# Second merge of an attention layer: kept branch weights, gates on GpSimd's queue, norm rows split between ScalarE and GpSimd

## The chip, the cores and the metric

The kernel runs on one core of one Trainium2 chip. The metric is the device time of one execution in microseconds (us). Three runs of the kernel before gave 1576.5, 1585.75 and 1576.89, median 1576.89. The profile is of one further execution of 1572.65 us.

## The reference

One layer over a sequence of 1024 rows with 1024 columns. It norms x, projects it, and runs two attentions of 8 heads each (a causal one with forget gates and one over chunks), whose outputs o_a and o_c have 512 columns each. What matters here is the part after that:

```python
merged = (jax.nn.sigmoid(gate_a) * (o_a @ w_br_fox[l])
          + jax.nn.sigmoid(gate_c) * (o_c @ w_br_chunk[l]))
mix = merged @ w_out[l]
x = _layer_norm(alpha * x + (1.0 + g1) * mix, ln1_g[l], ln1_b[l])
h = _layer_norm(x) * (1.0 + sc2) + sh2
...
```

Behind it follow an up-projection, a causal convolution of width 3, a gated product, a down-projection and a last norm. All is float32.

## The kernel before, in words

A float32 operand is held as a high and a low part, and a product is three matmuls: high by high, high by low, low by high (`mm3`, lines 192 to 194: L192, L193, L194). The tile framework's scheduler sets the order of each engine's instructions from the program, and adds the waits. A tile of a pool with `bufs=n` waits until the tile n allocations earlier under the same tag was read for the last time.

The sequence goes in two halves of 512 rows. Each half has a **merge** and a **mix**.

`merge(half)` makes the merged columns, transposed, in eight blocks c of 128 columns. A block has two branches (b=1, then b=0), each 12 matmuls into one PSUM bank `psb`: 24 per block, 192 per merge. Its weights are `brd[c]`, 1 MB in DRAM, loaded by `parted_w` (L904) as two transfers of 512 KB, the high parts into `wh` and the low parts into `wl`, every third time both into `ws`. Its gates are a tile of 512 KB, `sgl`, from `gd` (L914, two buffers). VectorE (DVE in the profile) multiplies each branch by its gate and so frees the bank (L921), adds the two (L927); ScalarE (ACT) rounds the sum to the high part `mh` (L930) and VectorE takes the low part `ml` (L931).

`mix(half)` multiplies the eight blocks, as k = 0 to 7, by the output weights `wod[k]` (again 512 KB twice): for four row tiles t of 128 rows two banks `psm` each, three matmuls per k and bank (L947 to L949), 192 in all. Banks for t = 0 to 2 come from the six that the merge uses in turn; those for t=3 are two others. The second mix does k=0 for all four t first, and then for each t the list k = 1, 2, 4, 5, 6, 7, 3. Behind each t, VectorE multiplies by g1 and adds alpha times the row tile of x, `xr` (L974, L975; `xr` is loaded at L965, four buffers).

`norms(half)` is the layer norm of the four row tiles: statistics (L119, L121), a small chain for the factor r (L123 to L132), then two VectorE operations over 128x1024: (x − mean) × l1g (L984) and × r + l1b (L985). GpSimd's queue (POOL) stores the row (`xd`, L987). Then the rows are normed once more for the FFN: statistics, and a scaling by ScalarE into `x2` (L139, L140). The norms of half 0 run beside merge 1, one step per block; those of half 1 behind mix 1. Behind mix 1 PE also turns the normed rows of half 0 (L997, `turned_0`) and starts the up-projection.

In merge 1 all loads are issued by SyncE's queue (SP): branch weights, gates, ln rows, and output weights for mix 1. GpSimd has only the `xd` stores and two loads of up-projection weights (L871) there. The pool `hap` holds `h_11` and `h_21`, sixteen tiles of 256 KB, which `turned_0` fills after merge 1; the space is unused until then.

Of the kernel before, what the change touches and what calls it, by code (L numbers as in the profile page):

```python
# [12 lines left out]
F32 = mybir.dt.float32  # L13
F32R = mybir.dt.float32r
AF = mybir.ActivationFunctionType
ALU = mybir.AluOpType
# [3 lines left out]
P = 128  # L20
# [3 lines left out]
KD = D // P  # L24
H = 512
# [19 lines left out]
def body(ctx, tc, a, out):  # L45
    nc = tc.nc
    ve, se, pe, po, sy = nc.vector, nc.scalar, nc.tensor, nc.gpsimd, nc.sync
    uid = [0]

    def nm(s):  # L50
        uid[0] += 1
        return f"{s}_{uid[0]}"

    def opened(**kw):
        cm = tc.tile_pool(reuse_waits="tile", **kw)
        return cm, cm.__enter__()
# [28 lines left out]
    gd = dram.tile([2, 16, P, H], F32, name="gd", tag="gd")  # L85
# [11 lines left out]
    brd = dram.tile([KD, 4, P, H], F32, name="brd", tag="brd")  # L97
# [17 lines left out]
    def norm_scale(src, n=2, st=None):  # L115
        if st is None:
            st = small.tile([P, n, 6], F32, name=nm("st"), tag=f"st{n}", bufs=4 if n == 2 else 1)
            for i in range(n):
                ve.bn_stats(out=st[:, i, :], in_=src[:, i * D // n : (i + 1) * D // n])  # L119
# [12 lines left out]
        ve.tensor_tensor(out=r, in0=y, in1=t, op=ALU.mult)  # L132
        return mv, r

    def normalise(dst, src, on_act=False, st=None):
        mv, r = norm_scale(src, 2, st)
        if on_act:
            b = small.tile([P, 1], F32, name=nm("nb"), tag="nb")
            ve.scalar_tensor_tensor(out=b, in0=mv[:, 0:1], scalar=-1.0, in1=r, op0=ALU.mult, op1=ALU.mult)  # L139
            se.activation(out=dst, in_=src, func=AF.Identity, scale=r, bias=b)  # L140
        else:
            ve.tensor_scalar(out=dst, in0=src, scalar1=mv[:, 0:1], scalar2=r, op0=ALU.subtract, op1=ALU.mult)
# [48 lines left out]
    def mm3(ps, wh, wl, xh, xl, start, stop):  # L191
        pe.matmul(ps, wh, xh, start=start, stop=False)  # L192
        pe.matmul(ps, wh, xl, start=False, stop=False)  # L193
        pe.matmul(ps, wl, xh, start=False, stop=stop)  # L194
# [530 lines left out]
    for u, (ip, _) in enumerate(plan):  # L725
# [5 lines left out]
        for n in range(8 * u, 8 * u + 8):  # L731
            ip, i, g = steps[n]
# [73 lines left out]
    def operands(pool, name):  # L806
        return [[pool.tile([P, H], F32R, name=f"{name}{c}{k}", tag=f"{name}{c}{k}") for c in range(2)] for k in range(4)]

    ha_cm, hap = opened(name="ha", bufs=1)
    h_11, h_21 = operands(hap, "ha"), operands(hap, "hb")  # L810
    mxp = ctx.enter_context(tc.tile_pool(name="mxp", bufs=6, space=PSUM, reuse_waits="tile"))
    mxt_cm, mxt = opened(name="mxt", bufs=2, space=PSUM)
    mxb_cm, mxb = opened(name="mxb", bufs=2)
# [81 lines left out]
    if True:  # L895
# [3 lines left out]
        def parted_w(src, pool=None):  # L899

            tags = ("wh", "wl") if pool or next(sets) % 3 < 2 else ("ws", "ws")
            parts = [(pool or wp).tile([P, 2, H], F32R, name=nm(g), tag=g) for g in tags]
            for x, j in zip(parts, (2, 0)):
                sy.dma_start(out=x.bitcast(F32), in_=src[j : j + 2].rearrange("j p n -> p j n"))  # L904
            return parts

        def merge(half, os_, beside, ahead=iter(())):
            ms = []
            held = {}

            def branch(c, b):
                if c not in held:
                    sg = mx.tile([P, 2, H], F32, name=nm("sgl"), tag="sgl", bufs=2)
                    sy.dma_start(out=sg, in_=gd[half, 2 * c : 2 * c + 2].rearrange("b p s -> p b s"))  # L914
                    held[c] = [x.rearrange("p j (k n) -> p (j k) n", k=4) for x in parted_w(brd[c])], sg
                (bh, bl), sg = held[c]
                ps = mxp.tile([P, H], F32, name=nm("psb"), tag="mm")
                for k in range(4):
                    kk = 4 * b + k
                    mm3(ps, bh[:, kk, :], bl[:, kk, :], os_[kk][0], os_[kk][1], k == 0, k == 3)  # L920
                ve.scalar_tensor_tensor(out=sg[:, b, :], in0=sg[:, b, :], scalar=1.0, in1=ps, op0=ALU.add, op1=ALU.mult)  # L921

            for c in range(KD):
                branch(c, 1)
                branch(c, 0)
                sg = held.pop(c)[1]
                ve.tensor_tensor(out=sg[:, 0, :], in0=sg[:, 0, :], in1=sg[:, 1, :], op=ALU.add)  # L927
# [3 lines left out]
                ve.tensor_sub(out=ml, in0=sg[:, 0, :], in1=mh)  # L931
                ms.append((mh, ml))
                next(ahead, None)
                next(beside, None)
            return ms
# [44 lines left out]

        def norms(half, xs, xn):
            for t, xx in enumerate(xs):
                mv, r = norm_scale(xx)
                ve.scalar_tensor_tensor(out=xx, in0=xx, scalar=mv[:, 0:1], in1=l1g, op0=ALU.subtract, op1=ALU.mult)  # L984
                ve.scalar_tensor_tensor(out=xx, in0=xx, scalar=r, in1=l1b, op0=ALU.mult, op1=ALU.add)  # L985
                yield
                po.dma_start(out=xd[4 * half + t], in_=xx)  # L987
            for xx in xs:
                x2 = mxb.tile([P, D], F32, name=nm("x2"), tag="x2", bufs=4)
                normalise(x2, xx, True)  # L990
                xn.append(x2)
                yield

        def turned(tiles, j, psp=mxt, tag="tt"):
            ps = psp.tile([P, H], F32, name=nm("pst"), tag=tag)
            for t in range(4):
                pe.transpose(ps[:, t * P : (t + 1) * P], tiles[t][:, j * P : (j + 1) * P], ident)  # L997
            h32 = mxb.tile([P, H], F32, name=nm("h32"), tag="h32", bufs=4)
            se.activation(out=h32, in_=ps, func=AF.Identity, scale=modc[:, 4 * KD + j : 4 * KD + j + 1],
                          bias=modc[:, 3 * KD + j : 3 * KD + j + 1])  # L1000
            return h32

        def put(dst, x, y=None, op=None, e=(ve, ve, po), pool=mxb, n=2):
            if y is not None:
                t = pool.tile([P, H], F32, name=nm("ht"), tag="ht", bufs=n)
                e[0].tensor_tensor(out=t, in0=x, in1=y, op=op)
                x = t
            (e[1].copy if e[1] is se else e[1].tensor_copy)(out=dst[0], in_=x)
            e[2].tensor_sub(out=dst[1], in0=x, in1=dst[0])
            return x  # L1010

        def turned_0(tiles):
# [22 lines left out]
        l1g = mx.tile([P, D], F32, name="l1g", tag="l1g", bufs=1)  # L1035
        l1b = mx.tile([P, D], F32, name="l1b", tag="l1b", bufs=1)
# [19 lines left out]
            pass  # L1056
        o_cm.__exit__(None, None, None)
        hd_cm, hdp = opened(name="hd", bufs=2, side="right")
        turning = turned_0(x0)
        xs1 = mix(1, m1, iter(()), wide, turning, hdp)  # L1060
        for _ in turning:
# [227 lines left out]
    with tc.tile_pool(name="dn", bufs=2, reuse_waits="tile") as dn:  # L1289
# [44 lines left out]
        for p in products:  # L1334
            ps = bank_b if p in ("P5", "P3", "P2") else bank_a
# [117 lines left out]
```

## Time and profile before

| | |
|---|---|
| median of three runs | 1576.89 us |
| profiled execution | 1572.65 us |
| its span, first to last instruction | 1570.9 us |
| TensorE busy, share of the span | 96% |
| VectorE, ScalarE, GpSimd | 69%, 45%, 41% |
| mean granted TensorE clock | 0.990 |
| merge 0 and mix 0 | 730 to 817 us |
| merge 1 | 817.1 to 870.2 us |
| mix 1 | 870.2 to 916.1 us |

A matmul row's duration is from its start to a modelled end, and matmuls overlap: the pace is read from the distance of the starts. Operations of VectorE overlap by some tens of nanoseconds too. A bracket behind a row is the idle time before it on its engine, and what ended that. For a DMA, the row on its queue is only the issue; the time from issue to landing stands apart. PE is TensorE's matmuls, PEld its weight loads.

### The profile page before, as it was taken

The numbers are of one execution on the slowest core, as the hardware profiler recorded it, in microseconds if no ns is written. First come the engines' busy times: TensorE is split into PE (matmuls) and PEld (weight loads), VectorE is DVE, ScalarE is ACT, GpSimd is POOL, SyncE is SP. The second block draws the span as 40 slices with busy tenths as digits, with TensorE's granted clock in tenths as the row PEclk, the third lists the DMA queues.
The fourth block names the chain that finished last, engine by engine and source line by source line (L and its number), as shares of the span: only waits on it lengthen the run. The fifth ranks groups of instructions, "written<-read, shape, count | busy, mean of one in ns | idle before, by whom it ended". The sixth has DMA issues, their size and how long they took to land.

```text
span 1570.9 us, 21838 instructions
## 1 busy us (share of the span) xinstructions
PE 1509.7 (96%) x7663; PEld 1268.5 (81%) x7663; DVE 1081.9 (69%) x2161; ACT 708.2 (45%) x1316; POOL 641.5 (41%) x579
## 2 busy tenths in 40 slices
PE   6999989999999999899998999999999999999996
PEld 3788788889888888788886887888888888788885
DVE  6747566567757676564449488677778876845798
ACT  3545444554445454342102256445454454555451
POOL 0038988888788876100000003545445453000000
PEclk9999999999999999999999999999999999999999
DMA  9156665756666788426999676344333332697552
GB/s 370 40 168 221 216 207 198 233 194 201 220 202 201 253 280 273 172 99 228 307 339 336 242 255 207 104 173 155 133 121 120 129 112 103 223 342 256 196 187 76
DMA packets 130399, 317.81 MB, mean 202 GB/s; under 512 B 12897, under 2 KB 21809, under 8 KB 130289
## 3 DMA queue, kind: packets, MB, share of 16 engines
q1 hardware_dynamic: 94192, 207.79, 39.5%
q0 software_dynamic: 24432, 88.88, 16.6%
q10 hardware_dynamic: 11664, 19.75, 3.4%
q8 instruction: 60, 0.98, 0.3%
q14 instruction: 51, 0.41, 0.1%
HBM read 223.73 MB, written 84.25 MB: 196 GB/s over the span
## 4 chain that ended last, share of the span: by engine, by line
PE 80%; DVE 9%; DMA 7%; issue 2%; ACT 1%; SPq 0%; DVEq 0%; ACTq 0%
PE psu L852 24%; PE pso L502 4%; PE psd L1270 4%; PE psd L1271 4%; PE psd L1269 4%; PE pst L488 3%; PE psg L192 3%; PE psg L193 3%; PE psg L194 3%; PE psq L193 3%; PE psq L194 3%; PE psq L192 3%; DMA cb<-in_rel_t 2%; PE pss L434 2%; PE pss L435 2%; PE psv L295 2%
## 5 line engine op out<-in xcount | busy, mean ns | idle before, releaser
L852 PE MATMUL psu<-hc,wx 128*128 128x512 f32 x792 | 185.7, 389 | 0.1
L852 PEld LDWEIGHTS psu<-hc,wx 128*128 128x128 f32 x792 | 148.6, 188 | 31.4 <-ACT u L1195 0.5
L1118 DVE SCALAR_TENSOR_TENSOR pcv<-u,convp,pcv 128x1024 f32<-128x1024 f32 x88 | 113.2, 1286 | 45.4 <-ACT pcv L1116 44.5
L454 ACT ACTIVATE s<-s,mx 128x640 f32<-128x640 f32 (+7 forms) x128 | 94.5, 738 | 78.6 <-DVE mx L448 77.0
L1259 DVE TENSOR_TENSOR op<-rw,op 128x512 fp32r<-128x512 f32 x146 | 93.3, 688 | 52.9 <-ACT op L1258 52.6
L1258 ACT CAST op<-rw 128x512 fp32r<-128x512 f32 x146 | 85.2, 623 | 84.3 <-PE psd L1271 40.8
L1270 PE MATMUL psd<-op,op 128*128 128x512 f32 x292 | 113.6, 389 | 1.0 <-DVE op L1259 1.0
L1271 PE MATMUL psd<-op,op 128*128 128x512 f32 x292 | 113.6, 389 | 0.0
L491 ACT CAST pt<-pst 128x512 fp32r<-128x512 f32 (+1 forms) x192 | 82.5, 450 | 68.8 <-PE pst L488 67.3
L1269 PE MATMUL psd<-op,op 128*128 128x512 f32 x292 | 113.1, 389 | 0.0
L987 POOL DMA_DIRECT2D xd<-xr x8 | 4.3, 542 | 263.1 <-DVE xr L985 263.1
L192 PE MATMUL psq<-h1h,wh 128*128 128x512 f32 x256 | 104.4, 409 | 1.7 <-DVE h1h L188 1.3
L492 DVE TENSOR_TENSOR pt<-pst,pt 128x512 fp32r<-128x512 f32 (+1 forms) x192 | 96.5, 519 | 13.2 <-ACT pt L491 11.3
L192 PE MATMUL psg<-h1h,wh 128*128 128x512 f32 x256 | 104.6, 409 | 0.0
L194 PE MATMUL psg<-h1h,wl 128*128 128x512 f32 x256 | 100.6, 393 | 1.5 <-DVE wl L112 1.5
L194 PE MATMUL psq<-h1h,wl 128*128 128x512 f32 x256 | 101.2, 395 | 0.9 <-DVE wl L112 0.9
L193 PE MATMUL psq<-h1l,wh 128*128 128x512 f32 x256 | 101.5, 396 | 0.0
L193 PE MATMUL psg<-h1l,wh 128*128 128x512 f32 x256 | 100.7, 393 | 0.0
L502 PE MATMUL pso<-pt,vs 128*128 128x256 f32 x608 | 93.2, 292 | 6.4 <-DVE pt L492 6.2
L550 POOL TENSOR_SCALAR dr<-dr,cond 128x512 f32<-128x512 f32 x56 | 95.7, 1711 | 5.1 <-DMA dr<-in_w_ada 4.1
L502 PEld LDWEIGHTS pso<-pt,vs 128*128 128x128 f32 x608 | 82.9, 194 | 15.2 <-DVE pt L492 8.5
L488 PE MATMUL pst<-ident,s 128*128 128x128 f32 x528 | 83.7, 275 | 8.9 <-DVE pt L492 8.7
(284 smaller groups left out, 4013.7 us busy)
## 6 DMA issues: line engine op xcount, KB each, us to landing
ws<-in_w_up SPq DMA_DIRECT2D x34, 512.0 KB, 3.8
dr<-in_w_ada POOLq DMA_DIRECT2D x32, 512.0 KB, 4.7
dr<-in_w_down POOLq DMA_DIRECT2D x22, 512.0 KB, 5.2
td<-dr POOLq DMA_DIRECT2D x22, 512.0 KB, 5.4
rw<-td SPq DMA_DIRECT2D x44, 256.0 KB, 4.6
yd<-y SPq DMA_DIRECT2D x20, 512.0 KB, 2.8
rw<-yd SPq DMA_DIRECT2D x40, 256.0 KB, 4.6
rw<-sd SPq DMA_DIRECT2D x33, 256.0 KB, 4.6
```

The costliest lines, as they stand in the source:

```text
L192: pe.matmul(ps, wh, xh, start=start, stop=False)
L193: pe.matmul(ps, wh, xl, start=False, stop=False)
L194: pe.matmul(ps, wl, xh, start=False, stop=stop)
L488: pe.transpose(ps[:, b * P : (b + 1) * P], st[:, c0 : c0 + P], ident)
L492: ve.tensor_sub(out=dl, in0=src, in1=dh)
L502: pe.matmul(ps[:, 0:256], vs[:, h % 2, j0 + j, :], pt[j // 4][:, c, j % 4, :], start=j == 0 and c == 0, stop=j == nj - 1 and c == 1)
L550: po.tensor_scalar_mul(x[:, k % 2, :] if k else acc, x[:, k % 2, :], cond[:, k : k + 1])
L852: pe.matmul(ps, w[:, a_, k, :], h[k][b_], start=first, stop=k == 3 and a_ == 1, skip_group_check=on)
L1118: ve.scalar_tensor_tensor(out=ps, in0=u[b][:, 2 - d : S + 2 - d], scalar=cp[:, 2 - d : 3 - d], in1=ps, op0=ALU.mult, op1=ALU.add)
L1269: pe.matmul(ps[t], g[:, 0, ts], d[:, 0], start=start, stop=False, skip_group_check=on)
L1270: pe.matmul(ps[t], g[:, 0, ts], d[:, 1], start=False, stop=False, skip_group_check=on)
L1271: pe.matmul(ps[t], g[:, 1, ts], d[:, 0], start=False, stop=stop, skip_group_check=on)
```

## The change

Three things are changed, all around merge 1.

1. **Branch weights of blocks 4 to 7 are kept.** In merge 0 they are loaded as sixteen tiles `kw` of 256 KB (new function `kept_w`, L915) into the space of `h_11` and `h_21`, whose allocation moves behind merge 1. Merge 1 uses them again, and takes the blocks in the order 4, 5, 6, 7, 0, 1, 2, 3. Only blocks 0 to 3 are loaded again there.
2. **Gates of merge 1** are issued by GpSimd's queue instead of SyncE's (L926).
3. **Norm rows:** for the four tiles of half 0 and the first two of half 1, ScalarE now applies mean and factor in one operation (`normalise` with `on_act`), and GpSimd multiplies by l1g and adds l1b, two operations of 128x1024 (L1001, L1002). The last two tiles of half 1 stay on VectorE as before (L1005, L1006).

```diff
-    h_11, h_21 = operands(hap, "ha"), operands(hap, "hb")
+    kept = {}
...
+        def kept_w(c):
+
+            if c not in kept:
+                kept[c] = []
+                for i, j in enumerate((2, 0)):
+                    kept[c].append([])
+                    for b in range(2):
+                        x = hap.tile([P, H], F32R, name=nm("kw"), tag=f"h{'ab'[c % 2]}{i}{2 * b + c // 2 % 2}")
+                        sy.dma_start(out=x.bitcast(F32), in_=brd[c, j + b])
+                        kept[c][i].append(x.rearrange("p (k n) -> p k n", k=4))
+            return kept[c]
+
...
-                    sy.dma_start(out=sg, in_=gd[half, 2 * c : 2 * c + 2].rearrange("b p s -> p b s"))
-                    held[c] = [x.rearrange("p j (k n) -> p (j k) n", k=4) for x in parted_w(brd[c])], sg
+                    (po if half else sy).dma_start(out=sg, in_=gd[half, 2 * c : 2 * c + 2].rearrange("b p s -> p b s"))
+                    if c >= 4:
+                        held[c] = kept_w(c), sg
+                    else:
+                        held[c] = [[x[:, j].rearrange("p (k n) -> p k n", k=4) for j in range(2)]
+                                   for x in parted_w(brd[c])], sg
...
-            for c in range(KD):
+            for c in (4, 5, 6, 7, 0, 1, 2, 3) if half else range(KD):
...
         def norms(half, xs, xn):
             for t, xx in enumerate(xs):
-                mv, r = norm_scale(xx)
-                ve.scalar_tensor_tensor(out=xx, in0=xx, scalar=mv[:, 0:1], in1=l1g, op0=ALU.subtract, op1=ALU.mult)
-                ve.scalar_tensor_tensor(out=xx, in0=xx, scalar=r, in1=l1b, op0=ALU.mult, op1=ALU.add)
+                if half == 0 or t < 2:
+                    normalise(xx, xx, True)
+                    po.tensor_tensor(out=xx, in0=xx, in1=l1g, op=ALU.mult)
+                    po.tensor_tensor(out=xx, in0=xx, in1=l1b, op=ALU.add)
+                else:
+                    mv, r = norm_scale(xx)
+                    ve.scalar_tensor_tensor(out=xx, in0=xx, scalar=mv[:, 0:1], in1=l1g, op0=ALU.subtract, op1=ALU.mult)
+                    ve.scalar_tensor_tensor(out=xx, in0=xx, scalar=r, in1=l1b, op0=ALU.mult, op1=ALU.add)
                 yield
                 po.dma_start(out=xd[4 * half + t], in_=xx)
...
+        h_11, h_21 = operands(hap, "ha"), operands(hap, "hb")
         turning = turned_0(x0)
```

How it moves instructions is seen at two places. First GpSimd's queue during merge 1. Row tiles t = 0 to 3 of half 0 are xr_8663, xr_8665, xr_8667, xr_8669; before, its part there is

```order
L987 DMA xd<-xr_8663 128x1024 [waits DVE_49]
L987 DMA xd<-xr_8665 128x1024 [waits DVE_49]
L987 DMA xd<-xr_8667 128x1024 [waits DVE_49]
L987 DMA xd<-xr_8669 128x1024 [waits DVE_49]
L871 DMA sgl_9505<-in_w_up 128x1024 [waits DMASW1_49,DMASW0_49,DVE_49]
```

and now, from the fifth gate on (sgl_8919, sgl_8979, sgl_9042 and sgl_9105 are the gates of blocks 0, 1, 2 and 3; the first four gates and all of tile 0 stand ahead):

```order
L1001 TENSOR_TENSOR xr_8665<-xr_8665,l1g 128x1024 [waits DMAHW2_49,Activation_49]
L926 DMA sgl_8919<-gd 128x2x512 [waits DMASW6_49,DMASW1_49,DVE_49]
L1002 TENSOR_TENSOR xr_8665<-xr_8665,l1b 128x1024 [waits Pool_49]
L1008 DMA xd<-xr_8665 128x1024 [waits DMASW2_49,Pool_49]
L1001 TENSOR_TENSOR xr_8667<-xr_8667,l1g 128x1024 [waits DMAHW2_49,DMAHW1_49,Activation_49]
L1002 TENSOR_TENSOR xr_8667<-xr_8667,l1b 128x1024 [waits Pool_49]
L1001 TENSOR_TENSOR xr_8669<-xr_8669,l1g 128x1024 [waits DMAHW6_49,Activation_49]
L1008 DMA xd<-xr_8667 128x1024 [waits DMASW3_49,Pool_49]
L1002 TENSOR_TENSOR xr_8669<-xr_8669,l1b 128x1024 [waits Pool_49]
L926 DMA sgl_8979<-gd 128x2x512 [waits DMASW7_49,DVE_49]
L926 DMA sgl_9042<-gd 128x2x512 [waits DMASW1_49,DVE_49]
L926 DMA sgl_9105<-gd 128x2x512 [waits DMASW4_49,DVE_49]
```

The gates of blocks 1, 2 and 3 now stand behind the work on all four rows. Second, VectorE at the end of merge 1: before, the row operations of the last tile stand between the evictions of a block (sgl_8923 is the gate tile of the fifth block),

```order
L921 SCALAR_TENSOR_TENSOR sgl_8923<-sgl_8923,psb_8929 128x512 [waits DMAHW5_49,PE_49]
L931 TENSOR_TENSOR ml_8901<-sgl_8865,mh_8900 128x512 [waits Activation_49]
L123 TENSOR_SCALAR v_8910<-mv_8908 128x1 [waits DVE_49]
L127 RECIPROCAL y_8914<-sd_8912 128x1 [waits Activation_49]
L984 SCALAR_TENSOR_TENSOR xr_8669<-xr_8669,mv_8908,l1g 128x1024
```

and now, behind the fifth block's low part (ml_8955), the second norm's statistics wait for GpSimd's last row, and the evictions of blocks 1, 2 and 3 follow in a row:

```order
L947 TENSOR_TENSOR ml_8955<-sgl_8919,mh_8954 128x512 [waits Activation_49]
L139 SCALAR_TENSOR_TENSOR nb_9039<-mv_9026,r_9037 128x1 [waits DVE_49]
L121 BN_AGGR mv_9089<-st_9086 128x2
L119 BN_STATS st_9145<-xr_8669 128x6 [waits Pool_49]
...
L937 SCALAR_TENSOR_TENSOR sgl_8979<-sgl_8979,psb_8985 128x512 [waits DMASW4_49,PE_49]
L937 SCALAR_TENSOR_TENSOR sgl_8979<-sgl_8979,psb_8999 128x512 [waits PE_49]
L943 TENSOR_TENSOR sgl_8979<-sgl_8979 128x512 [waits DVE_49]
L947 TENSOR_TENSOR ml_9015<-sgl_8979,mh_9014 128x512 [waits Activation_49]
L937 SCALAR_TENSOR_TENSOR sgl_9042<-sgl_9042,psb_9048 128x512 [waits DMASW6_49,PE_49]
```

VectorE no longer does the row operations, but it now waits for GpSimd in their place, and block 3's gate needs the buffer that ml_9015 frees.

More of the change, by code (lines that the diff above doesn't have):

```diff
@@ L905, in parted_w @@
             return parts
+        def kept_w(c):
[8 more added lines that the diff above has]
+            return kept[c]
         def merge(half, os_, beside, ahead=iter(())):
-            ms = []
+            ms = {}
             held = {}
@@ L918, in branch @@
                 for k in range(4):
-                    kk = 4 * b + k
-                    mm3(ps, bh[:, kk, :], bl[:, kk, :], os_[kk][0], os_[kk][1], k == 0, k == 3)
+                    oh, ol = os_[4 * b + k]
+                    mm3(ps, bh[b][:, k, :], bl[b][:, k, :], oh, ol, k == 0, k == 3)
                 ve.scalar_tensor_tensor(out=sg[:, b, :], in0=sg[:, b, :], scalar=1.0, in1=ps, op0=ALU.add, op1=ALU.mult)
-            for c in range(KD):
+            for c in (4, 5, 6, 7, 0, 1, 2, 3) if half else range(KD):
                 branch(c, 1)
@@ L931, in merge @@
                 ve.tensor_sub(out=ml, in0=sg[:, 0, :], in1=mh)
-                ms.append((mh, ml))
+                ms[c] = (mh, ml)
                 next(ahead, None)
```

## Prediction

> **What bounds the kernel now.** I read the windows first, cut at the first and last matmul of each stage around the change: merge 0 with mix 0, merge 1, mix 1. Columns: window, length, then busy time and count of each engine, granted clock, DMA share, GB/s.
>
> ```profile
> core 0: us, PE busy (x) PEld busy (x) DVE busy (x) ACT busy (x) POOL busy (x), PEclk, DMA share, GB/s
> 817.09:870.18 53.09, 47.64 (x194) 37.38 (x192) 46.84 (x114) 12.20 (x20) 2.72 (x5) 0.94 0.93 342
> 870.18:916.12 45.94, 45.65 (x210) 37.57 (x209) 26.84 (x53) 10.21 (x18) 1.61 (x3) 1.00 0.59 218
> 730.00:817.00 87.00, 87.00 (x385) 72.03 (x385) 35.85 (x48) 9.77 (x13) 0.00 (x0) 1.00 0.98 320
> ```
>
> Merge 0 and mix 0 keep PE busy without a break: 385 matmuls in 87.00 us, 0.226 us each. Merge 1 has 192 of the same matmuls, 43.5 us at that pace, and takes 53.09: **9.6 us are lost there**, the only stage of the three that loses much. Next the matmul rows of merge 1 around each gap (start, time, operation, in brackets the idle time and its releaser):
>
> ```profile
> 845.54 0.39 PE L193 MATMUL psb<-ol,wh 128*128 128x512 f32 x1
> 847.44 0.50 PE L194 MATMUL psb<-oh,wl 128*128 128x512 f32 x1 [1.51 <-DMA wl<-brd]
> ...
> 857.82 0.39 PE L194 MATMUL psb<-oh,wl 128*128 128x512 f32 x1
> 860.74 0.47 PE L192 MATMUL psb<-oh,ws 128*128 128x512 f32 x1 [2.52 <-DVE st L119]
> ...
> 861.83 0.63 PE L193 MATMUL psb<-ol,ws 128*128 128x512 f32 x1
> 863.43 0.80 PE L194 MATMUL psb<-oh,ws 128*128 128x512 f32 x1 [0.98 <-DMA ws<-brd]
> ...
> 865.73 0.63 PE L193 MATMUL psb<-ol,ws 128*128 128x512 f32 x1
> 866.16 0.63 PE L194 MATMUL psb<-oh,ws 128*128 128x512 f32 x1
> ...
> 868.14 0.39 PE L192 MATMUL psb<-oh,ws 128*128 128x512 f32 x1
> ...
> 870.18 0.39 PE L947 MATMUL psm<-wh,mh 128*128 128x512 f32 x1
> 872.90 0.39 PE L947 MATMUL psm<-wh,mh 128*128 128x512 f32 x1
> ```
>
> And SyncE's queue, which issues these weights (start, time in the queue):
>
> ```profile
> 852.96 0.43 SPq L904 DMA_DIRECT2D ws<-brd  x1
> 857.76 0.36 SPq L914 DMA_DIRECT2D sgl<-gd  x1
> 858.22 0.42 SPq L904 DMA_DIRECT2D ws<-brd  x1
> ```
>
> The three gaps, start to start less one matmul, are 1.67, 2.69 and 1.17 us, with some tenths at 823: about 6.3. All are branch weights that come late; the 2.52 is put down to DVE, but the first matmul of `ws` starts 7.8 us after that load's issue at 852.96, so it is the load again. The remaining 3 us are pace: after the gaps matmuls start 0.43 apart instead of 0.23, until 868.1. So the stage is bound by 8 MB of branch weights, 4 MB of gates and the loads beside them, at a DMA share of 0.93.
>
> **The change, part by part.**
>
> *Weights kept.* Blocks 4 to 7 need no load in merge 1: 4 of its 8 MB are gone, and the other four blocks, now last, are asked for early. All gaps above go, and the half pace behind them. Merge 1's matmuls would end at 817.09 + 43.5 = 860.6, **−9.6 us**, if nothing else held them. The same loads in merge 0 become 16 of 256 KB instead of 8 of 512 KB: the bytes are equal, eight more issues at about 0.4 us each stand in SyncE's queue, and PE is covered there by weights that arrive ahead. I take 0, and the uncovered price for the third rival.
>
> *Gates behind GpSimd's work.* In merge 1 a gate tile is now issued by GpSimd's queue, which also does the four rows' scaling and adding. In GpSimd's order the gate of block 1 stands behind all eight of these operations, and those of 2 and 3 behind it. An eviction of a block needs its gate, and mix 1 needs the banks: t=2's first matmul (872.90 above) waits until block 3's product is evicted. So the chain is: tile 0 scaled by ACT, eight GpSimd operations and four issues, block 1's gate, its evictions, block 3's gate into the same buffer, its eviction, t=2. Rows for its terms:
>
> ```profile
> 829.94 0.15 DVE L132 TENSOR_TENSOR r<-y,t 128x1 f32<-128x1 f32 x1
> ...
> L984 DVE SCALAR_TENSOR_TENSOR xr<-xr,mv,l1g 128x1024 f32<-128x1024 f32 x4 | 5.1, 1271 | 0.0
> L140 ACT ACTIVATE x<-xr,nb,r 128x1024 f32<-128x1024 f32 x4 | 5.0, 1242 | 4.4 <-DVE nb L139 4.4
> L927 DVE TENSOR_TENSOR sgl<-sgl 128x512 f32<-128x512 f32 x8 | 5.5, 682 | 0.0
> L921 DVE SCALAR_TENSOR_TENSOR sgl<-sgl,psb 128x512 f32<-128x512 f32 x16 | 10.7, 675 | 5.9 <-PE psb L194 3.1 <-DMA sgl<-gd 2.8
> L931 DVE TENSOR_TENSOR ml<-sgl,mh 128x512 fp32r<-128x512 f32 x7 | 4.8, 689 | 0.3
> L987 POOL DMA_DIRECT2D xd<-xr x4 | 2.2, 547 | 208.7 <-DVE xr L985 208.7
> ```
> ```profile
> L553 POOL TENSOR_TENSOR acc<-acc,dr 128x512 f32<-128x512 f32 x56 | 73.5, 1313 | 1.5
> ```
> ```profile
> sgl<-gd SPq DMA_DIRECT2D x16, 512.0 KB, 5.9
> dr<-in_w_ada POOLq DMA_DIRECT2D x32, 512.0 KB, 4.7
> ```
> ```profile
> DMA to landing us min/median/max: 3.6/5.9/10.5
> ```
>
> No 128x1024 operation of two tensors on GpSimd stands in this trace. The nearest row is the same operation over 512 columns, 1313 ns. Twice that is 2.63. From below: VectorE's step from 512 to 1024 columns is 675 to 1271 ns, a factor of 1.88, which gives 2.47. From above: such an operation of GpSimd takes 1.75 instead of 1.29 in the stretch where VectorE works on two SBUF operands at once,
>
> ```profile
> 978.86 1.75 POOL L841 TENSOR_TENSOR wl<-s,wl 128x512 fp32r<-128x512 f32 x1
> ...
> 983.51 1.29 POOL L841 TENSOR_TENSOR wx<-wt,wx 128x512 fp32r<-128x512 f32 x1
> ```
>
> so 3.5. I take **2.63**, since the 1313 is a mean over 56 in company of a working VectorE. The working: tile 0's factor is there at 830.1; ACT takes it after the cast in its way, about 832.0, and needs 1.24: 833.2. Eight operations are 21.0, four issues of 0.55 are 2.2: block 1's gate is issued at 856.4. The landing was 5.9 from SyncE's queue in a crowded stretch and 4.7 for the same size from GpSimd's: I take 5.3, 861.7. Two evictions, the sum, ACT's cast and the low part, with VectorE operations starting 0.60 apart, are 3.1: the buffer is free at 864.8. Issue 0.2, landing 5.3, eviction 0.7: **t=2 starts at 871.0, 1.9 us before its 872.90 of now**. The 9.6 us thus shrink to 1.9: what was bought in weights is spent waiting for gates.
>
> *Pace after the wait.* Between 860.6 and 871.0 PE has only the first two row tiles of mix 1, 12 matmuls, 2.7 us. That is an idle stretch longer than those of now, after which matmuls ran at half pace from 861.4 to 868.1, 13 or 14 of them at 0.2 us extra each: **+2.7 us** here, at the start of the rest of mix 1. The Trainium skill, "TensorE: Matmul & The Clock Gate", Part 1, says that the clock halves after an idle window of about 3.4 us and returns after 3.4 us of work; an estimate by it is 1.7 us lost, so the sum would be −0.7 instead; the trace already shows half pace after a gap of 2.5.
>
> *Mix 1's own wait* is a weight that is late in the queue behind the branch weights,
>
> ```profile
> 883.10 0.50 PE L948 MATMUL psm<-wl,mh 128*128 128x512 f32 x1 [0.29 <-DMA wl<-wod]
> ```
>
> start to start 0.7, less one matmul: **−0.5**.
>
> *VectorE* loses eight operations of 1.27 in half 0 (10.2 us) and gains four of 0.15, but its operations on two SBUF tensors may slow beside GpSimd:
>
> ```profile
> L838 DVE TENSOR_TENSOR wt<-ws,ws x14: 677/1651/1781, 979.4 to 1305.8; 128x512 f32<-128x512 f32 x14
> ```
>
> 677 ns at best, 1651 in the middle (minimum/median/maximum). Two of these per block (sum, low part) over five blocks are at most 10 × 1.0 us. The two nearly cancel, VectorE has 6 us of slack in the stage, and GpSimd is done before the links of the chain that run on VectorE: 0. The Trainium skill, "GPSIMD Engine Reference", sections 1 and 3.1, speaks against the move: GpSimd shares its SBUF interface with VectorE instructions of two SBUF inputs, and an addition of two tensors over 2048 columns took 4497 ns. An estimate from that for 1024 is 2.25 us alone; the sum would be −2.7. The rows here are slower for their size than that.
>
> *SyncE* loses eight gate issues from merge 1, but the row loads of half 1 now wait for ACT to have read a tile that GpSimd finished, and the weights of k=1 and k=2 of mix 1 are queued behind them. GpSimd ends its last tile at about 856, statistics and ACT take it to 860; before, these weights went out at
>
> ```profile
> 870.14 0.87 SPq L904 DMA_DIRECT2D ws<-wod  x2
> ```
>
> so they are earlier all the same: 0.
>
> *Half 1.* Four VectorE operations go (two row tiles),
>
> ```profile
> 901.11 1.26 DVE L984 SCALAR_TENSOR_TENSOR xr<-xr,mv,l1g 128x1024 f32<-128x1024 f32 x1
> ...
> 909.34 1.23 DVE L985 SCALAR_TENSOR_TENSOR xr<-xr,r,l1b 128x1024 f32<-128x1024 f32 x1
> ```
>
> all under mix 1's matmuls, which end at 916. What PE waits for later comes from the last row tile, still on VectorE. From 0 to 5 us could be in it if these tiles became late on GpSimd; it has 2.6 × 2 each and nothing else to do. I take 0.
>
> **Sum** against the profiled execution (1572.65): −1.9 + 2.7 − 0.5 = +0.3, so 1573.0. Its median of three runs, 1576.89, lies 4.2 above: **1577 us**, no change. About 1% (15.8 us) is what a measurement of this kernel can tell from none, and no case below reaches it on its middle value.
>
> **The rivals.**
>
> *The gates come in time.* GpSimd at 2.47 ends 1.3 us earlier, and with less traffic both gates could land in the 3.6 of the fastest: −3.4. Then t=2 starts at 866.3, 6.6 before now; with the 0.5 of mix 1 that is −7.1, or 1570; without any half pace. If ACT comes earlier by 1 to 2 us as well, −9, 1568. For it: the DMA share falls with 4 MB less. Against it: GpSimd's eight operations are a fixed row, and even block 1's gate cannot be issued before 855.
>
> *Slower: GpSimd and VectorE get in each other's way.* At 3.5 each, eight operations take 28.0, 7.0 more than forecast; every microsecond of them goes on to block 1's gate: t=2 at 878.0, sum +7.3, **1584**. With slow landings of about 7.5 twice, 4.4 more: 1588. It decides from where GpSimd's operation passes 2.63: the forecast stands at no change, so each 0.1 us above costs 0.8. For it: the 1.75 row and VectorE's 1651. Against it: VectorE reads PSUM in half its work here, and the 1313 is a mean taken in company.
>
> *The change doesn't do what it says*: the kept loads, twice as many issues, come too late in merge 0, whose DMA share is already 0.98. Eight further issues of 0.42 are 3.4 us in the queue, and with a half pace after the gap about +5: 1582 with the forecast's rest. Against it: PE never waits there now.
>
> **How the numbers follow.** Forecast 0.45 (its own range 1573 to 1581); gates in time 0.25; slower by contention 0.2; stalls in merge 0, 0.1. The range from 1567 to 1588 takes in their ends. Over 1% faster would be below 1561, more than all that merge 1 loses, 0.02; over 1% slower, above 1592.7, needs GpSimd operations of 4.6 us, 0.03; within, 0.95.
>
> **What would show it.** Right: merge 1 has no wait for brd; GpSimd's 128x1024 operations take 2.5 to 2.7; the first matmul of t=2 starts within 2 us of 871 after a wait for a VectorE eviction that itself waited for a gate; half-pace matmuls follow. Wrong: t=2 starts before 868 (gates free), after 874 (contention), or merge 0 shows waits for `kw`; or the stretch behind 916 moves by more than 2 us.

## The result and the profile after

The changed kernel takes 1587.66 us, the median of 20 runs (1575.97 to 1599.25), against 1576.76 for the kernel before, also of 20: ratio **1.0079, 95% interval 1.0054 to 1.0103**, slower by 8.5 to 16 us. The forecast was no change. Its profiled execution took 1579.61 us with a span of 1577.5, 6.6 more than the 1570.9 of before.

The windows of the change, cut as those of before (merge 1, the wait behind it, mix 1; the last number of a row is GB/s, the share ahead of it that of the DMA engines, then the granted clock):

```profile
core 0: us, PE busy (x) PEld busy (x) DVE busy (x) ACT busy (x) POOL busy (x), PEclk, DMA share, GB/s
816.16:864.06 47.90, 45.63 (x193) 36.83 (x191) 46.95 (x96) 13.67 (x20) 25.43 (x17) 0.96 0.57 198
864.06:870.32 6.26, 0.15 (x2) 0.03 (x1) 5.11 (x13) 3.13 (x4) 0.74 (x1) 0.73 1.02 400
870.32:923.35 53.03, 49.78 (x208) 38.91 (x209) 25.94 (x53) 12.55 (x20) 11.88 (x8) 0.93 0.57 211
```

From the first matmul of merge 1 to the end of mix 1 (called the **stage** from here on) it took 99.0 us before (817.09 to 916.12) and 107.2 now (816.16 to 923.35). Merge 1 is 5.2 shorter, 6.3 of waiting stand behind it, and mix 1 is 7.1 longer: +8.2. What lies behind the stage is 654.2 us now and 654.8 before, so half 1's rows on GpSimd cost nothing. The rows at the gaps:

```profile
859.62 0.50 PE L192 MATMUL psb<-oh,wh 128*128 128x512 f32 x1 [2.27 <-DVE sgl L937]
...
870.32 0.77 PE L963 MATMUL psm<-wh,mh 128*128 128x512 f32 x1 [6.11 <-DMA wh<-wod]
871.56 0.79 PE L964 MATMUL psm<-wl,mh 128*128 128x512 f32 x1 [0.47 <-DMA wl<-wod]
...
877.74 0.50 PE L963 MATMUL psm<-wh,mh 128*128 128x512 f32 x1 [1.12 <-DVE sgl L937]
883.06 0.50 PE L964 MATMUL psm<-wl,mh 128*128 128x512 f32 x1 [0.68 <-DMA wl<-wod]
889.76 0.50 PE L964 MATMUL psm<-wl,mh 128*128 128x512 f32 x1 [0.92 <-DMA wl<-wod]
```

No gap waits for `brd` any more: the kept weights do what they say. Instead there are two new ends. The weights of k=0 of mix 1 come late, and SyncE's queue shows why:

```profile
843.79 0.41 SPq L904 DMA_DIRECT2D wl<-brd  x1
860.27 3.18 SPq L981 DMA_DIRECT2D xr<-in_x  x2
863.54 0.40 SPq L904 DMA_DIRECT2D wh<-wod  x1
```

After the last branch weight the queue stands still for 16 us, until ScalarE has read the first row tile (860.24); the second row load goes out when it has read the next (863.08), and only then the weights of k=0. And t=2's first matmul at 877.74 waits for a gate, as forecast, but later. Cut there, mix 1 has two parts (columns as above):

```profile
870.32:877.74 7.42, 5.82 (x12) 3.73 (x13) 1.44 (x3) 0.37 (x1) 0.57 (x1) 0.53 1.04 396
877.74:923.35 45.61, 43.96 (x196) 35.18 (x197) 24.51 (x51) 12.18 (x19) 11.31 (x7) 1.00 0.50 181
```

The half pace (granted clock 0.53) lies ahead of t=2's first matmul, beside the wait for the gate; behind it the clock is 1.00. From the start of merge 1 to that matmul it was 55.8 us before and is 61.6 now, +5.8; from there to the end of mix 1 it was 43.2 and is 45.6, +2.4, most of it the waits for output weights at 883.06 and 889.76. The chain of waits that ends at t=2's first matmul (start, duration, what):

```profile
842.27 2.98 DVE t L129
845.24 0.12 DVE mv L121
...
846.94 1.25 ACT xr L140
848.20 0.08 issue
848.28 2.38 POOL xr L1001
...
850.74 1.28 POOL xr L1002
852.01 1.08 issue
853.09 2.85 POOL xr L1001
...
856.51 2.30 POOL xr L1002
858.81 4.88 DMA sgl<-gd
...
868.57 8.34 DMA sgl<-gd
...
877.00 0.70 DVE sgl L937
```

The first step is the one to look at. `t` at L129 is an operation on one column of 128 rows; the forecast's own rows have such operations at 0.15 us. Here it took 3. VectorE's and GpSimd's rows side by side:

```profile
842.19 3.05 DVE L129 SCALAR_TENSOR_TENSOR t<-y,v 128x1 f32<-128x1 f32 x1
...
848.42 2.26 DVE L139 SCALAR_TENSOR_TENSOR nb<-mv,r 128x1 f32<-128x1 f32 x1
...
851.33 2.35 DVE L947 TENSOR_TENSOR ml<-sgl,mh 128x512 fp32r<-128x512 f32 x1
...
856.54 2.37 DVE L139 SCALAR_TENSOR_TENSOR nb<-mv,r 128x1 f32<-128x1 f32 x1
```
```profile
842.82 2.40 POOL L1002 TENSOR_TENSOR xr<-xr,l1b 128x1024 f32<-128x1024 f32 x1
...
848.28 2.38 POOL L1001 TENSOR_TENSOR xr<-xr,l1g 128x1024 f32<-128x1024 f32 x1 [2.08 <-ACT xr L140]
850.74 2.40 POOL L1002 TENSOR_TENSOR xr<-xr,l1b 128x1024 f32<-128x1024 f32 x1
853.09 2.85 POOL L1001 TENSOR_TENSOR xr<-xr,l1g 128x1024 f32<-128x1024 f32 x1
...
856.51 2.37 POOL L1002 TENSOR_TENSOR xr<-xr,l1b 128x1024 f32<-128x1024 f32 x1
```

842.19 + 3.05 is 845.24, and GpSimd's operation ends at 845.22. 848.42 + 2.26 is 850.68, GpSimd's end 850.66. So it goes on, with one difference by size: the 128x512 row ends at 853.68, 0.54 behind GpSimd's 853.14. **A VectorE operation that reads two tensors from SBUF doesn't get through until GpSimd's operation ends**, however small it is. It goes both ways: GpSimd's next operation, at 853.09, took 2.85 instead of 2.4, while that 128x512 row ran out. What the starts do not explain is the 842.19 row: it began 0.6 us before GpSimd's operation, while GpSimd was issuing a gate's load (842.03 to 842.80). Evictions of 128x512 that take one operand from PSUM (L937) and the statistics (L119) pass at their usual 0.6 to 0.7. Busy time of VectorE hides this: 46.95 us in merge 1, as before, though 8 large operations are gone.

### The profile page after: what moved, and what is told of

Its sections match the earlier page's. It is cut to its first block, busy times and chain, and to the rows that moved or that the text cites. A ratio compares the mean times of both kernels' runs of the same rounds, so it can differ in the third digit from the quotient of the medians.

```text
span 1577.5 us, 21858 instructions
## 1 busy us (share of the span) xinstructions
PE 1511.4 (96%) x7663; PEld 1267.5 (80%) x7663; DVE 1084.5 (69%) x2155; ACT 714.9 (45%) x1322; POOL 676.5 (43%) x599
## 4 chain that ended last, share of the span: by engine, by line
PE 77%; DVE 11%; DMA 7%; issue 2%; ACT 2%; POOL 1%; SPq 0%; DVEq 0%; POOLq 0%; ACTq 0%
PE psu L852 24%; PE psd L1292 4%; PE psd L1293 4%; PE psd L1291 4%; PE pso L502 4%; PE pst L488 3%; PE psg L192 3%; PE psg L193 3%; PE psg L194 3%; PE psq L192 3%; PE psq L194 2%; PE psq L193 2%; DMA cb<-in_rel_t 2%; PE pss L434 2%; PE psv L295 2%
## 5 line engine op out<-in xcount | busy, mean ns | idle before, releaser
L1281 DVE TENSOR_TENSOR op<-rw,op 128x512 fp32r<-128x512 f32 x146 | 93.2, 686 | 53.0 <-ACT op L1280 52.8
L926 POOL DMA_DIRECT2D sgl<-gd x8 | 5.9, 738 | 195.4 <-DVE sgl L937 128.6
```

## The experiments

Three theories were set against each other. **Hold**: VectorE's operations on two SBUF tensors wait while GpSimd works, and everything on VectorE is late. **Gates**: the gates stand behind GpSimd's rows. **SyncE's order**: weights stand behind row loads that wait. Stages are read from the first matmul of merge 1 and the last of mix 1, one profiled execution each (three of the kernel before lie 2.1 us apart, three of the change 0.2); ratios are to the kernel before.

| run | stage us | ratio, 95% interval |
|---|---|---|
| before | 99.0 | 1 |
| the change | 107.2 | 1.0079 (1.0054 to 1.0103) |
| e1 row loads on ScalarE's queue | 108.6 | 1.0070 (1.0039 to 1.0102) |
| e2 gates on SyncE's queue | 104.4 | 1.0025 (0.9999 to 1.0051) |
| e3 norm rows on VectorE | 95.3 | 0.9977 (0.9952 to 1.0002) |
| e4 kept weights alone | 93.0 | 0.9972 (0.9948 to 0.9996) |
| e5 norm rows alone | 107.8 | 1.0056 (1.0032 to 1.0080) |
| e6 rows in four pieces | 107.0 | 1.0060 (1.0028 to 1.0092) |
| e7 one tensor read | 106.4 | one run |
| e8 two row operations on VectorE | 93.6 | 0.9964 (0.9937 to 0.9990) |
| e9 GpSimd busy beside kept weights | 97.4 | 1.0014 (0.9991 to 1.0037) |
| e10 e8, t=3 first | 93.2 | 0.9973 (0.9948 to 0.9998) |
| e11 e8, three gate buffers | 90.7 | 1.0005 (0.9978 to 1.0032) |
| e12 e10 and e11 | 90.5 | 1.0002 (0.9976 to 1.0029) |
| e13 both queues freed | 102.7 | 1.0032 (1.0004 to 1.0059) |
| e14 e13 with rows on VectorE | 98.7 | 0.9998 (0.9965 to 1.0030) |
| e15, e16 the change again | 107.4, 107.4 | one run each |
| e17, e18 before again | 99.7, 97.6 | one run each |

### One queue at a time, and the parts alone

**e1**, row loads of half 1 on ScalarE's queue:

```diff
-                sy.dma_start(out=xx, in_=a["x"][tt * P : (tt + 1) * P, :])
+                (se if half else sy).dma_start(out=xx, in_=a["x"][tt * P : (tt + 1) * P, :])
```

> As the change, but the four loads of half 1's row tiles are issued by ScalarE's queue, so that SyncE's queue has the weights of k=0 straight behind the branch weights. Stage = first matmul of merge 1 to last of mix 1: 99.0 us before, 107.2 with the change. Theory 'SyncE's order' (row loads that wait for ScalarE stand ahead of the weights): the 6.1 us wait at the start of mix 1 goes and the stage falls to 100 or 101. Theory 'gates': t=2 of mix 1 still waits for block 3's gate until about 877 on the trace of the change, so only 1 to 2 us go, 105 to 106. Theory 'VectorE held by GpSimd': the same 105 to 106, since block 3's gate is late because VectorE was.

Stage 108.6. The wait for k=0's weights is gone; 2.25 us of waiting for ScalarE stand in its place, and t=2 waits longer for its gate:

```profile
876.50 0.80 PE L963 MATMUL psm<-wh,mh 128*128 128x512 f32 x1 [7.31 <-DVE sgl L937]
```

SyncE's order alone is not the cause; it lay over another wait that ended no earlier. No theory had expected more than 106.

**e2**, gates back on SyncE's queue:

```diff
-                    (po if half else sy).dma_start(out=sg, in_=gd[half, 2 * c : 2 * c + 2].rearrange("b p s -> p b s"))
+                    sy.dma_start(out=sg, in_=gd[half, 2 * c : 2 * c + 2].rearrange("b p s -> p b s"))
```

> As the change, but the gates of merge 1 are issued by SyncE's queue again. Theory 'gates' (they stand behind GpSimd's operations): the stage falls from 107.2 to below 98. Theory 'SyncE's order': one row load still stands ahead of the weights of k=0 and waits for ScalarE, so mix 1 starts at about 54 us after the start of merge 1 as now; 105 to 107. Theory 'VectorE held by GpSimd': the evictions and the norm chain stay late, 103 to 107.

104.4, so the gates' place on GpSimd alone is not it either. A gate waits for a buffer that VectorE frees, and SyncE's branch weights now stand behind it:

```profile
864.30 0.77 PE L192 MATMUL psb<-oh,wh 128*128 128x512 f32 x1 [3.58 <-DMA wh<-brd]
...
885.14 0.77 PE L963 MATMUL psm<-wh,mh 128*128 128x512 f32 x1 [3.46 <-DMA wh<-wod]
```

**e3** and **e4**: `norms` as in the kernel before, e4 with e2's edit besides.

> As the change, but all norm rows on VectorE again; kept weights and the gates on GpSimd's queue stay. All three theories lose their cause here. The stage should be 99.0 less the 9.6 us of late branch weights, 89 to 91, and the time about 1567; if it stays above 97, the cause is none of the three but the kept weights or their order.

> Kept weights and their order alone: gates on SyncE's queue, norm rows on VectorE. If the queue of the gates matters by itself, this differs from the run with gates on GpSimd's queue and norm rows on VectorE by more than 1 us in the stage; if only what stands ahead of them on GpSimd matters, the two are equal, 89 to 91.

95.3 and 93.0: with the rows on VectorE the stage falls by 12 to 14 us, to less than before. It stays above the 89 to 91 expected, since in both merge 1 runs without a break but t=2 then waits for block 3's eviction, with half pace behind it (e4):

```profile
812.41:855.93 43.52, 43.52 (x193) 36.05 (x192) 39.45 (x86) 7.91 (x14) 2.19 (x4) 1.00 0.82 291
```
```profile
861.10 0.50 PE L963 MATMUL psm<-wh,mh 128*128 128x512 f32 x1 [2.29 <-DVE sgl L937]
```

Whether the gates go by GpSimd or SyncE is 2 us between two single executions and nothing in the ratios.

**e5**, the kernel before with the new `norms` alone:

> The kernel before with the norm rows of the change alone (no kept weights, gates on SyncE's queue, no row loads ahead of the weights of k=0). Theory 'VectorE held by GpSimd': its cost does not need the other two edits, the stage (first matmul of merge 1 to last of mix 1, 99.0 before) grows by 4 to 9 us and the time by about as much. Theory 'queues' (the GpSimd rows hurt only by what stands behind them on GpSimd's and SyncE's queue): neither is there, 97 to 100.

107.8: +8.8 without the other two edits; without a hold 97 to 100 was expected. VectorE's rows are long again, and here SyncE hands it on, since the gates there wait for VectorE with branch weights behind them:

```profile
835.55 2.35 DVE L139 SCALAR_TENSOR_TENSOR nb<-mv,r 128x1 f32<-128x1 f32 x1
```
```profile
867.41 0.79 PE L194 MATMUL psb<-oh,wl 128*128 128x512 f32 x1 [3.80 <-DMA wl<-brd]
```

### The hold itself

**e6**, each GpSimd operation in four of 256 columns:

```diff
+                    for i in range(4):
+                        s4 = slice(256 * i, 256 * (i + 1))
-                    po.tensor_tensor(out=xx, in0=xx, in1=l1g, op=ALU.mult)
-                    po.tensor_tensor(out=xx, in0=xx, in1=l1b, op=ALU.add)
+                        po.tensor_tensor(out=xx[:, s4], in0=xx[:, s4], in1=l1g[:, s4], op=ALU.mult)
+                        po.tensor_tensor(out=xx[:, s4], in0=xx[:, s4], in1=l1b[:, s4], op=ALU.add)
```

> As the change, with each of GpSimd's 128x1024 operations cut into four of 128x256; the queues stay in the change's order. Theory 'VectorE is held until the running GpSimd instruction ends': VectorE's rows of 2 to 3 us in merge 1 (also those of 128x1) shrink to below 1 us, the norm chain runs ahead and the stage falls from 107.2 to 100 to 104. Theory 'shared bandwidth': the rows stay about as long in sum, stage 106 to 110.

107.0, and the longest VectorE row became longer, not shorter:

```profile
852.97 5.72 DVE L132 TENSOR_TENSOR r<-y,t 128x1 f32<-128x1 f32 x1
```
```profile
853.07 1.44 POOL L1003 TENSOR_TENSOR xr<-xr,l1g 128x256 f32<-128x256 f32 x2
854.47 1.42 POOL L1004 TENSOR_TENSOR xr<-xr,l1b 128x256 f32<-128x256 f32 x2
855.85 1.42 POOL L1003 TENSOR_TENSOR xr<-xr,l1g 128x256 f32<-128x256 f32 x2
857.24 1.43 POOL L1004 TENSOR_TENSOR xr<-xr,l1b 128x256 f32<-128x256 f32 x2
```

Eight pieces in a row, and VectorE gets through at 858.69, when the row of them ends (858.67). A second 128x1 row took 4.27, also to the end of a row of pieces; both began while GpSimd was issuing a row's store. Five others, of 0.58 to 0.78, came through at the end of a single piece with the next one behind it in four of them. So my form of the theory (until the running instruction ends) fell as a rule: a back-to-back row of GpSimd instructions can hold VectorE to its end. When it does is not settled. That each of these rows ends within 0.03 us of the end of a piece speaks for a hold and against shared bandwidth. The stage stayed long by SyncE's order too: the weights of k=0 let PE wait 10.4 us here.

**e7**, GpSimd reading one tensor: both operations became `po.tensor_scalar_mul(xx, xx, ones[:, 0:1])`; the kernel leaves out l1g and l1b, so it doesn't compute the layer.

> As the change, but GpSimd's two operations read one tensor and multiply by a column of ones (the multiplication by l1g and the addition of l1b are left out); the queues stay in order. If the hold comes from GpSimd instructions of two tensors, VectorE's long rows are gone (0.15 for 128x1, 0.69 for 512 columns) although GpSimd's operations take 2.4 to 3.4 each. If any GpSimd instruction holds VectorE, the rows grow with them to 2 to 3.4 us, and the stage to 107 or more.

Neither expectation held as written. GpSimd took 2.85 each, and VectorE was held, but only for the first part:

```profile
849.52 1.52 DVE L132 TENSOR_TENSOR r<-y,t 128x1 f32<-128x1 f32 x1
```
```profile
849.90 2.86 POOL L1002 TENSOR_SCALAR xr<-xr,ones 128x1024 f32<-128x1024 f32 x1
```

VectorE goes on at 851.04, 1.14 into an operation of 2.86; the other 128x1 rows give 1.12 to 1.15, and a low part of 512 columns ends at 1.67. The stage stayed at 106.4: GpSimd's rows took longer, the weights of k=0 stood behind the row loads and let PE wait 8.5 us, and t=2 waited 2.6 more for its gate. For the division of the loss this run decides nothing.

**e8**, the same two operations issued by `ve` instead of `po`, all else as in the change:

> As the change, with the two operations of a row on VectorE instead of GpSimd (ScalarE still applies mean and factor, gates still on GpSimd's queue). It keeps the longer chain of a row (ScalarE, then two operations) and takes GpSimd's work away. Theory 'VectorE held by GpSimd': stage 93 to 97, as with the old norm rows (95.3). Theory 'the row's longer chain': still above 102.

93.6 and a ratio of 0.9964 (0.9937 to 0.9990). The longer chain of a row costs nothing; GpSimd's part does. The operation takes 1.2 us there, half of GpSimd's 2.4:

```profile
L1001 DVE TENSOR_TENSOR xr<-xr,l1g x6: 1209/1222/1227, 834.0 to 901.1; 128x1024 f32<-128x1024 f32 x6
```

**e9**, e4 with GpSimd busy in merge 1 on something nobody waits for:

```diff
+                if half and c >= 4:
+                    for i in range(4):
+                        x = mx.tile([P, H], F32, name=nm("dummy"), tag="dummy", bufs=1)
+                        po.tensor_tensor(out=x, in0=mh.bitcast(F32), in1=mh.bitcast(F32), op=ALU.mult)
```

> The kernel with kept weights alone (gates on SyncE's queue, norm rows on VectorE; its stage 93.0 us), and beside it sixteen 128x512 products of GpSimd in merge 1, four behind each of the first four blocks' high parts, into a tile that nobody reads: about 19 us of GpSimd's time with no gate behind it (only row stores and two later loads). Theory 'VectorE held by GpSimd': VectorE gets rows of 1 to 5 us and the stage grows to 97 to 104. Theory 'queues' (GpSimd's work hurts only by what waits for it): 92.5 to 94.

97.4 against e4's 93.0, at the lower end of what the hold theory expected; VectorE's low parts took up to 1.52 instead of 0.69:

```profile
838.96 1.52 DVE L947 TENSOR_TENSOR ml<-sgl,mh 128x512 fp32r<-128x512 f32 x1
```

Nothing on PE's path waits for this work, so about 4.4 us is what the hold does by itself, as far as two single executions tell; the ratios, 1.0014 (from 0.9991) against 0.9972 (to 0.9996), point the same way, and their intervals overlap a little.

**e13**, e1 with the gates of merge 1 on ScalarE's queue too; **e14**, the same with e8's edit.

> As the change, but the gates of merge 1 and the row loads of half 1 are issued by ScalarE's queue, so that neither gates nor weights stand behind GpSimd's work or behind a row load; GpSimd still does the rows. Theory 'queues': stage within 2 us of the control with the rows on VectorE, 92 to 96. Theory 'VectorE held by GpSimd': evictions and the norm chain stay late by themselves, 99 to 105.

> The control of the former: the same queues, the two operations of a row on VectorE. Both theories: 92 to 95, as with the gates on GpSimd's queue (93.55).

102.7 and 98.7. Freeing both queues takes 4.5 of the 107.2; taking GpSimd's work away takes another 4.0, near e9's 4.4. With free queues and GpSimd's rows the stage is where the hold theory had it (99 to 105), and not at the 92 to 96 of the queues. The control missed its 92 to 95: in it, output weights come late in mix 1 (waits of 0.75 and 2.94), so moving gates and row loads to ScalarE's queue has a price of its own, which is not traced further.

### Better than both

**e10**: k=0 of mix 1 in the order t = 0, 1, 3, 2 on top of e8. **e11**: three gate buffers on top of e8. **e12**: both.

> As the run with the two row operations on VectorE (stage 93.55, ratio 0.9964), and mix 1 takes k=0 for t=3 ahead of t=2, whose banks are the last to come free: six more matmuls (1.4 us) in front of the wait of 3.5. Stage 92 to 92.5; ratio 0.995 to 0.997.

> As the run with the two row operations on VectorE, with three gate buffers instead of two: block 3's gate waits for the low part of block 0, not of block 1, and is issued some 6 us earlier. If that gate is what t=2 waits for, the wait of 3.5 and the half pace behind it go: stage 89.5 to 91, ratio 0.993 to 0.996. If it is the eviction itself, 93.

> Both of the former together: stage 89 to 91, ratio 0.993 to 0.996; not faster than three gates alone if that takes the wait away.

e10's order moves the wait (2.42 instead of 3.51), and the stage gains 0.3, less than two executions can tell. e11 and e12 bring the stage to 90.7 and 90.5, as expected, and the time back to 1.0005 and 1.0002, which was not. Part of the gain is given back ahead of the stage: from the first matmul of merge 0 to that of merge 1 it is 87.0 before (730.1 to 817.09), 87.1 with the change, but 92.4 in e12 (731.0 to 823.42). Output weights of mix 0 come late there:

```profile
799.77 0.50 PE L964 MATMUL psm<-ws,mh 128*128 128x512 f32 x1 [1.06 <-DMA ws<-wod]
806.45 0.50 PE L964 MATMUL psm<-wl,mh 128*128 128x512 f32 x1 [0.95 <-DMA wl<-wod]
```

### The kept loads, three executions of each kernel

Such waits stood in the profiled executions of e3, e6 and e10 to e14, 1 to 6 us of merge 0 and mix 0, with none in before or e5, which keep no weights, and none over 0.3 us in the other kernels that keep them (the change, e1, e2, e4, e7, e8, e9). That would have been the prediction's third rival, and the medians of before and the change lie 10.9 us apart, more than the stage explains. So both kernels were profiled twice more:

> The change once more, for one thing: merge 0 and mix 0 (87.1 us in its first profiled execution, where nothing waits). If the kept weights bring mix 0 to the edge of its loads, some executions of the change show waits for output weights there and 88 to 93 us; if the waits of mix 0 in seven of the runs before came from their own edits, 87.0 to 87.1 again. The stage should be 106 to 109 in both cases.

> As the former, a further execution: 88 to 93 us in merge 0 and mix 0 by the edge of the loads in about half the executions, 87.0 to 87.1 if the edits of the other runs were the cause.

> The kernel before once more: merge 0 and mix 0 were 87.0. If kept weights cause the late output weights, 87.0 again; if every kernel has them now and then, 88 to 93 in some executions of this one too.

> As the former, a further execution: 87.0 if kept weights are the cause of the late output weights of mix 0.

Merge 0 and mix 0 took 87.0 to 87.1 in all four, without a wait: the change itself does not lose there. The stage is 107.2 to 107.4 in three executions of the change, and 97.6 to 99.7 in three of the kernel before. Why seven of the edited kernels stalled in mix 0 is not settled; in e12 and e11 SyncE issued output weights already at 720 and 731, before merge 0 began; in e3 and e6 it did not.

So the best here are e8, e4 and e10, 0.3% to 0.4% below before, with intervals that end between 0.9990 and 0.9998, and not told apart from each other or from e3.

## Why the prediction was wrong

- **Where the end would come from: right in place.** t=2's first matmul was forecast to wait for block 3's gate, behind the gate of block 1, behind GpSimd's rows. That is the chain of waits shown above. It was forecast 53.9 us after the start of merge 1 (871.0) and came 61.6 after (877.74): 7.7 too early, which is nearly the whole miss in the stage (+8.2 instead of +0.3). Along the chain, block 1's gate was issued 3.3 late and landed 0.4 faster than taken; from its landing to the issue of block 3's gate it took 1.8 more than forecast (4.9 against 3.1); and block 3's gate landed in 8.34 instead of 0.2 + 5.3, 2.8 more. The sign that the prediction itself gave for contention, t=2 after 874, is the one that came.
- **GpSimd's price: too high, harmlessly.** Taken as 2.63, measured 2.38 to 2.40, once 2.85. Eight of them are 1.5 shorter than forecast, and yet the gate of block 1 was issued 42.7 us into the merge instead of 39.3: from GpSimd's first operation (832.38) to that issue it took 26.4, not 21.0 + 2.2, since GpSimd stood waiting between them.
- **The step that failed is "*VectorE* ... The two nearly cancel ... 0".** It priced the meeting of the two engines as a slowing of two 512-column operations per block, at most 1.0 us each, beside slack, and took GpSimd to be done before the chain runs on VectorE. The runs showed a hold that takes any two-tensor operation, 128x1 too, to the end of GpSimd's operation. Six 128x1 rows of the change between 832 and 859 took 13.1 us in sum (0.15 to 0.2 each otherwise), two low parts 4.8 instead of 1.4. They lie in the serial chain of a row's factor, which feeds ScalarE, which feeds GpSimd, which holds the gates. The row quoted for it, 677/1651/1781, had the fact in it: the spread was read as a rate, not as a wait. One of those operations, in the kernel before,

```profile
979.37 1.78 DVE L838 TENSOR_TENSOR wt<-ws,ws 128x512 f32<-128x512 f32 x1
```

ends at 981.15, 0.54 behind the GpSimd operation that the prediction quotes at 978.86 with 1.75: the same distance as in the change. The Trainium skill, "SBUF — State Buffer", section "SBUF: two separate sides", says it outright: the pair of ports that the two engines share is an exclusive lock, whichever starts first holds it for the whole instruction, and a VectorE instruction with two SBUF inputs contends with GpSimd. The 848.42 row agrees (GpSimd began 0.14 before it); the 842.19 row, which began 0.6 before GpSimd's operation, doesn't fit "first" by the starts that the profile shows; e6's 5.72 over eight instructions goes beyond the page, and e7's 1.14 of 2.86 stays short of it.

- **The second step that failed is *SyncE*, "so they are earlier all the same: 0".** It named the weights of k=1 and k=2; the weights of k=0 stand behind two of the row loads as well. Issued at 863.54, they let PE wait 6.1 us. e1 shows that this alone decided nothing, since the gate held t=2 there until 64.6 us after the start of merge 1, later than the 61.6 of the change; with the rows on VectorE the scheduler put these weights ahead of the row loads anyway.
- **The landing of a gate was taken too short.** The 5.3 was the middle of 5.9 and 4.7; the gate of block 3 took 8.34, 8.26 and 8.23 in three executions of the change, with the DMA share at 1.04 from 870 to 878. It also took 8.14 in e3 and 8.29 in e8, which have the rows on VectorE, so the hold is not its cause. This is 2.8 of the 7.7.
- **Kept weights: right.** No wait for `brd`, no stall in merge 0 (87.0 to 87.1 in three executions), merge 1 in 43.5 us when nothing else holds it (e4). The gain by itself is 6.0 us of stage (99.0 against 93.0, one execution each), not 9.6 + 0.5; t=2 then waits for block 3's eviction.
- **Pace: wrong, and made good by luck.** +2.7 of half pace was forecast behind t=2's start. It came ahead of it, on the twelve matmuls of the first two row tiles (granted clock 0.53), where PE had to wait for the gate in any case; behind t=2 the clock was 1.00. Instead output weights came late twice, 0.85 and 1.08 us over a matmul's 0.23, where the forecast had such waits gone. So +2.4 stands against a forecast of +2.2 for this part, by another cause. Nor does the length of a gap alone give half pace: it followed gaps of 2.66 and 2.67 us, start to start (the change at 856.96, e4 at 858.42), and none followed one of 3.89 in e8.
- **Half 1 at 0: right** (654.2 against 654.8 behind the stage).
- **The rivals.** The slower one had the right two engines and the wrong victim: it let GpSimd's operation grow to 3.5, when GpSimd kept its pace and VectorE stood. Its 1584, and its 1588 with two slow landings, came nearest to the 1587.66; one slow landing did come, the slow GpSimd did not. The range to 1588 was drawn from that GpSimd of 3.5, so that it just takes in the result is luck. The stalls in merge 0 did not come.

What the loss is made of: the rows on GpSimd cost 13.6 us of stage (107.2 against e8's 93.6). The hold by itself is about 4 (e9, and e13 against e14), the two queues 4.5 (e13). The rest of the 13.6, about 5, is not separated: e14, with the rows on VectorE, was itself 5 above e8. All of these are differences of single executions. The stage explains 8.5 (107.3 against 98.8, means of three executions each) of a difference that the runs put at 8.5 to 16. The rest is not traced to anything: the part ahead of merge 0 ended at 729, 734 and 738 in three executions of the change and at 730, 736 and 738 in three of the kernel before, a spread as wide as the whole effect and no tendency in it.

## What to carry to other kernels

Before work is moved to GpSimd, list VectorE's operations that read two tensors from SBUF in the same stretch, and count for each, however small, a wait to the end of the GpSimd operation beside it, at worst to the end of a row of them (e6). Small ones in a serial chain cost most, and VectorE's busy share shows none of it as idle. A row of a view whose minimum and median lie far apart is to be asked what it waited for, and a queue is to be read down to the first instruction that PE needs, not only past it.

## What the runs showed of the hardware

A VectorE operation of 128x1 on two SBUF tensors took 1.57 to 3.05 us in six rows beside GpSimd's two-tensor operations of 2.4 (0.15 to 0.2 otherwise) and ended within 0.03 us of their end; one of 128x512 ended some 0.55 behind it. Beside pieces of 256 columns back to back two such rows took 4.27 and 5.72, five 0.58 to 0.78. Beside a GpSimd operation that reads one tensor (2.85 us) they went on after 1.12 to 1.15. In the change, operations with an operand in PSUM and statistics were not held (0.6 to 0.7).
